# A streaming encoder layer on one core: the orders at both borders of its MLP are changed

## The chip, the cores and the metric

The kernel runs on one core of a Trainium2 chip. The metric is the device time of one execution in microseconds, the median of several runs. A core has five engines that work side by side and wait for each other through semaphores: TensorE (PE; its weight loads are PEld) multiplies matrices into PSUM, VectorE (DVE) and ScalarE (ACT) work element by element on SBUF and PSUM, GpSimd (POOL) does so on SBUF alone, and SyncE (SP) issues the transfers (DMA). Each engine takes its instructions in the order in which they stand for it.

## What is computed

One layer of an encoder on 1024 prompt rows and 64 sample rows of 1024 numbers: an input projection, three groups of heads, an output projection, a layer norm, and then the part that matters here, an MLP with a squared ReLU and the second norm:

```python
def sq_relu_mlp(x, w_up, w_down):
    h = jnp.square(jax.nn.relu(jnp.einsum('btd,df->btf', x, w_up)))
    return jnp.einsum('btf,fd->btd', h, w_down)
...
        xp = layer_norm(ALPHA * xp + mix, ln1_g[l], ln1_b[l])
        xp = layer_norm(ALPHA * xp + sq_relu_mlp(xp, w_up[l], w_down[l]), ln2_g[l], ln2_b[l])
```

w_up is 1024 x 4096, w_down 4096 x 1024; all numbers are float32.

## The kernel before

**Precision.** Each factor of a product is kept as two parts: a high half, which an activation on ScalarE rounds into the multiplier's format, and a low half, what is left, which `lo_sub` (L98) subtracts on VectorE or GpSimd. A product runs three passes of matmuls: high by high, high by low, low by high. Making both halves of an operand is called a split (`split`; its activation stands at L1232).

**Seven products for eight.** Both matrices of the MLP are cut in quarters and multiplied by a scheme with seven products, whose operands are sums and differences of quarters, of the data and of the weights, and whose results are added and subtracted to the four quarters of the result.

**Up.** The 4096 columns of w_up are taken in 16 pairs of blocks, p = 0 to 15, each with two chains: s = 0 (288 columns of x, the samples among them) and s = 1 (256). `prep(p)` (L1489) loads the weights (`up_load`, tile wr), splits three blocks as they are into tile wa (`wops` 0, 1 and 3, for the products 0, 1 and 5), makes four sums in place (`w_sums`, L1241 to L1245) and splits these into tile ws: `high` is the activation (L1514), `low` the subtraction. A `Chain` runs products 0 to 6 in PSUM banks A, B, C and D; after each, VectorE adds the result into the eight-part tile hh (L1308 to L1314). Product 6 goes into the bank D that product 3 had, so it waits until L1308, which follows product 4, has read it. `relu` (L1326) and `sums` (L1335 to L1338) make the operands of down, and SP stores them in DRAM (h4_dr, h3_dr, hs_dr; L1339 to L1343). At the end of up, c3 is the chain of p = 15 with s = 1, and c4 the one with s = 0, the last of all.

**Down.** 4096 rows of w_down are taken in 8 parts c, each with two groups g of rows of x: g = 2c and 2c + 1. For a part, `wd_load` loads two tiles of raw rows, `wd_split(c, q, n)` splits its seven operands n, and `wd_sum(c, q, k)` (L1426) makes the four differences k in place: difference 3 is what split 6 reads, and split 3 reads difference 2. For a group, `h_load` fetches operands of h (which = 0: four, which = 1: three) and `h_split(g, which, x)` splits them over a PSUM tile st (L1453, L1457, L1458). `Down` runs seven products for two blocks of rows x, in PSUM banks that VectorE adds into `acc` (L1721 for the first addition to a bank's result, L1723 for others). `acc_load` (L1469) fetches rows of x into acc first. `sample` does the 64 sample rows by way of the tile hs, loaded by `hs_load`; `b12_again` reloads one block of weights (rb) for it.

**Where tiles lie.** acc 2 and 6 (tile a26) take the place of c4's tile hh0, and acc 3 and 7 (a37) that of c3's hh1: they can be loaded when c4's or c3's stores are through. Raw rows of part 0, q = 1, lie in the tile awa, and so does half of group 1's operands (`hraw[0, 1]`, in the place of two of those raw blocks) and acc NB, the samples' rows. hx, the other half of group 1's operands, has held operands of group 0. acc 1, 4 and 5 lie where up's operand x lay, and can be loaded behind the last product of up.

**The order.** A scheduler with a model of times orders each engine's instructions, except inside `in_order`, where the order of the text is kept on every engine. The stretches that the change touches are inside: the chains of p = 1 with `prep(2)` (for p = 2 TensorE's order alone), the last three chains of up, and `first_group`, which is group 0 of down. What follows `first_group` is the scheduler's, so instructions of group 1 may stand among those of group 0, and a change in one place may move others behind it.

Of the kernel before, what the change touches and what calls it, by code (L numbers as in the profile page):

```python
# [12 lines left out]
F32 = mybir.dt.float32  # L13
# [7 lines left out]
P = 128  # L21
PASSES = ((0, 0), (0, 1), (1, 0))
D = 1024
# [33 lines left out]
def _build(nc, tc, a, es):  # L57
# [39 lines left out]
    def lo_sub(eng, out, src, hi):  # L97
        eng.tensor_tensor(out, src, hi.bitcast(F32), op=ALU.subtract)  # L98
# [1132 lines left out]
    def split(hi, lo, raw, eng):  # L1231
        nc.scalar.activation(hi, raw, AF.Copy)  # L1232
        lo_sub(eng, lo, raw, hi)
# [189 lines left out]
    def wd_sum(c, q, k, eng):  # L1423
        r = raws[c, q]
        o, x, y = ((0, 1, 0), (1, 3, 1), (3, 3, 0), (2, 2, 3))[k]
        eng.tensor_tensor(r[:, o], r[:, x], r[:, y], op=ALU.subtract)  # L1426
# [20 lines left out]
    def h_split(g, which, x, only=None, qs=(0, 1)):  # L1447

        for q in qs:
            t = h_tile(g, which, x)  # L1450
            o = 3 if which else 4
            raw = t[:, 1, q].bitcast(F32) if (g, which) == (0, 0) else hraw[which, q][:, :, x * P:(x + 1) * P]
            nc.scalar.activation(t[:, 0, q], raw, AF.Copy)  # L1453
            tag = (only or ("o", "tr"))[n_stage[0] % 2]
            n_stage[0] += 1
            st = ps.tile([P, 4, P], F32, name=f"st{n_stage[0]}", tag=tag, bufs=1 if tag in ("o", "tr") else 2)[:, 0:o]
            nc.scalar.activation(st, t[:, 0, q].bitcast(F32), AF.Copy)  # L1457
            nc.vector.tensor_tensor(t[:, 1, q], raw, st, op=ALU.subtract)  # L1458
# [17 lines left out]
    def two(t, tile_):  # L1476
        accf[t] = tile_
        acc[t, 0], acc[t, 1] = tile_[:, 0:512], tile_[:, 512:D]

    with p3:  # L1480
# [7 lines left out]
        def prep(p, rest=True, raw=None):  # L1488
            raw = raw or up_load(p)  # L1489
            pool = rp if p % 2 else lp  # L1490
            wa = pool.tile([P, 3, 2, 4, P], F32R, name=f"wa{p}", tag="wa")
            f0, f1 = raw[0:2]
            a, b = slice(0, 4), slice(4, 8)
            for o, src in ((0, f0[:, a]), (1, f0[:, b]), (2, f1[:, b])):
                split(wa[:, o, 0], wa[:, o, 1], src, nc.gpsimd)
            whole = len(raw) == 3
            parts = ((slice(0, 256), raw[2]),) if whole else ((slice(0, P), f0), (slice(P, 256), f1))

            wsp = []

            def summed(part=(0, 1)):
                w_sums(f0, f1, part)
                if 1 not in part:
                    return
                ws = pool.tile([P, 2, KT, 256], F32R, name=f"ws{p}", tag="ws")
                wsp.append(ws)
                wops[p].update({2: ws[:, :, b, 0:P], 4: ws[:, :, b, P:256],
                                5: ws[:, :, a, 0:P], 6: ws[:, :, a, P:256]})

            def high():  # L1510
                ws = wsp[0]
                for q in (a, b) if whole else (slice(0, 8),):
                    for c, src in parts:
                        nc.scalar.activation(ws[:, 0, q, c], src[:, q], AF.Copy)  # L1514

            def low():
                ws = wsp[0]
                for c, src in parts:
                    lo_sub(nc.vector, ws[:, 1, :, c], src, ws[:, 0, :, c])

            wops[p] = {0: wa[:, 0], 1: wa[:, 1], 3: wa[:, 2]}
            if rest:
                summed()
                high()
                low()
            return summed, high, low
# [98 lines left out]
        def products(c, some):  # L1625
            for i in some:
                c.product(i, False)

        with in_order(border):
            c1 = chain(NP - 2, 1)  # L1630
            products(c1, (0, 1))
            ch.relu()
            products(c1, (2,))
            ch.sums()
            products(c1, (3, 4))
            summed()
            high()
            products(c1, (5, 6))
            c2 = chain(NP - 2, 0)
            products(c2, (0, 1))  # L1640
            c1.relu()
            c1.sums()
            products(c2, (2,))
            low()
            wd_load(0, 0)
            products(c2, (3, 4, 5, 6))
            c3 = chain(NP - 1, 1)
            products(c3, (0,))

            h4 = lp.tile([P, 2, 2, 2, 4, P], F32R, name="h4a", tag="ws")  # L1650
            hbuf[0, 0], hbuf[0, 1] = h4[:, 0], h4[:, 1]
            for q in range(2):
                for x in range(2):
                    nc.sync.dma_start(h4[:, x, 1, q].bitcast(F32), h4_dr[q, 0][:, :, x * P:(x + 1) * P])
            awa = lp.tile([P, 3, D], F32, name="awa", tag="wa")
            hx = lp.tile([P, D], F32, name="hx", tag="hx")
            hraw[0, 0], hraw[0, 1] = (y.rearrange("p (o c) -> p o c", o=4) for y in (hx, awa[:, 1]))
            two(0, awa[:, 2])

            two(NB, awa[:, 0])  # L1660
            h_load(0, 1, 0)
            wd_load(0, 1, awa[:, 0:2].rearrange("p q (o c) -> p (q o) c", o=2))
            products(c3, (1,))
            c2.relu()
            products(c3, (2,))
            c2.sums()
            acc_load(0)
            products(c3, (3, 4))
            h_split(0, 0, 0, ("o", "s"))
            products(c3, (5, 6))  # L1670
            c4 = chain(NP - 1, 0)
            products(c4, (0,))
            slots = [big.tile([P, 8704], F32R, name=f"wd0_{q}", tag="xw") for q in range(2)]
            for q in range(2):
                wset[0][q] = slots[q][:, 0:7168].rearrange("p (h b c) -> p h b c", h=2, b=7)
                hbuf[1, q] = slots[q][:, 7168:8704].rearrange("p (h q o c) -> p h q o c", h=2, q=2, o=3)

            def both_pairs(n):
                for q in range(2):
                    wd_split(0, q, n, nc.gpsimd)  # L1680

            both_pairs(0)
            products(c4, (1,))
            h_split(0, 0, 1, ("o", "s"))
            both_pairs(2)
            for q in range(2):
                wd_sum(0, q, 0, nc.vector)
            products(c4, (2,))
            both_pairs(1)
            wd_sum(0, 0, 1, nc.vector)  # L1690
            products(c4, (3, 4))
            wd_sum(0, 1, 1, nc.vector)
            products(c4, (5,))
            h_load(0, 1, 1)
            for q in range(2):
                wd_sum(0, q, 2, nc.vector)
            h_split(0, 1, 0, ("tr", "s"))
            both_pairs(3)
            products(c4, (6,))
            both_pairs(4)  # L1700
# [3 lines left out]
    with ExitStack() as p3:  # L1704
# [173 lines left out]
        def first_group():  # L1878
            ch = [Down(0, x) for x in range(2)]

            def both(n):
                for d in ch:
                    d.product(n)
                for d in ch:
                    d.evac(n)

            for t in (1, 4, 5):
                acc_load(t)
            for q in range(2):
                wd_sum(0, q, 3, nc.vector)  # L1890
            both(0)
            for q in range(2):
                wd_split(0, q, 5, nc.gpsimd)
            h_split(0, 1, 1)
            h_load(1, 0, 0)
            both(1)
            for q in range(2):
                wd_split(0, q, 6, nc.gpsimd)
            for q in range(2):
                h_load(1, 1, q)  # L1900
            both(2)
            h_split(1, 0, 0, None, (0,))
            c4.relu()
            both(3)
            h_load(1, 0, 1)
            wd_load(1, 0)
            c3.relu()
            both(4)
            h_split(1, 0, 0, None, (1,))
            c3.sums(nc.gpsimd)  # L1910
            c4.sums()
            h_split(1, 0, 1)
            both(5)
            a37 = lp.tile([P, 2, D], F32, name="acc37", tag="hh1")
            two(3, a37[:, 0])
            two(7, a37[:, 1])
            for t in (2, 6, 3, 7, NB):
                acc_load(t)
            for k in range(3):
                wd_split(1, 0, k, nc.gpsimd)  # L1920
            both(6)
            wd_sums(1, 0, nc.gpsimd)
            wd_split(1, 0, 3, nc.vector)
            wd_split(1, 0, 4, nc.gpsimd)
            wd_split(1, 0, 5, nc.vector)
            wd_split(1, 0, 6, nc.gpsimd)
# [207 lines left out]
```

## Time and profile before

| | |
|---|---|
| three runs, us | 1390.9, 1392.92, 1397.63 |
| median, us | 1392.92 |
| profiled execution, us | 1389.83 |
| its span, first to last instruction, us | 1388.1 |
| granted TensorE clock, mean | 0.988 |
| up, us from the start of the span | about 672 to 1026 |
| down, us from the start of the span | about 1026 to 1388 |

The profile has a page for the whole execution and answers to questions: groups of instructions, waits, windows, a timeline and the chain of work that ended last. In a timeline row stand the start in us, the busy time, engine, line, operation, tiles written <- tiles read, shapes, the number of instructions merged and, in brackets, how long the engine was free before and what it waited for. In a row of waits stand the waiting engine, line and tile, what it waited for, the total in us, how often, and the longest. The lines that matter stand in the prediction.

### The profile page before, as it was taken

What the parts mean: (1) busy time and instruction counts of PE and PEld (TensorE: products, weight loads), DVE (VectorE), ACT (ScalarE), POOL (GpSimd) and SP (SyncE); (2) the same over time, 40 slices, a digit from 0 to 9 for tenths busy, and PEclk for the clock granted to TensorE, in tenths of its full rate; (3) what the DMA queues carried; (4) which work ended last, traced back from release to release, by engine and by line L of the source; (5) the groups of instructions that cost most, each with busy time, mean ns of one, the idle gap of its engine ahead of it and who ended that gap; (6) DMA issues with size and microseconds to landing.
All of it is one profiled execution on the core that took longest, in us unless ns stands there. A gap on an engine that the chain in (4) does not pass through costs nothing.

```text
span 1388.1 us, 24324 instructions
## 1 busy us (share of the span) xinstructions
PE 1322.0 (95%) x8827; PEld 1203.3 (87%) x8827; DVE 998.1 (72%) x1795; ACT 719.1 (52%) x1561; POOL 612.3 (44%) x667
## 2 busy tenths in 40 slices
PE   7999999999898998999999999999998999999996
PEld 7899989999888997877899999999986788887874
DVE  4577666576788379779866878767677677768677
ACT  4367566566556366334523222222266676767665
POOL 3231231256665446756412212212167675565547
PEclk9999999999999999999999999999999999999999
DMA  7445474231403247532234344344468334334333
GB/s 221 111 123 152 154 212 116 68 78 43 103 13 74 62 153 250 169 107 76 77 114 143 124 163 141 119 169 141 159 217 291 119 142 167 130 129 158 109 126 129
DMA packets 159088, 185.64 MB, mean 134 GB/s; under 512 B 27756, under 2 KB 117164, under 8 KB 158968
## 3 DMA queue, kind: packets, MB, share of 16 engines
q1 hardware_dynamic: 158968, 184.08, 41.7%
q8 instruction: 70, 1.15, 0.3%
q14 instruction: 50, 0.41, 0.1%
HBM read 117.65 MB, written 60.10 MB: 128 GB/s over the span
## 4 chain that ended last, share of the span: by engine, by line
PE 52%; DVE 15%; DMA 10%; ACT 9%; POOL 9%; issue 5%; SPq 0%; ACTq 0%; DVEq 0%; POOLq 0%
PE zA L1294 9%; PE zD L1294 6%; PE kvsb L362 5%; PE kvfox L362 4%; PE mx L251 4%; POOL wd L98 3%; PE zC L1294 3%; PE zB L1294 3%; PE A L1756 3%; DMA rd<-w_down 3%; POOL rd L1426 2%; DVE snsb L545 2%; DMA rwo<-w_out 2%; DMA awa<-h_dr 2%; DMA raw<-w_in 1%
## 5 line engine op out<-in xcount | busy, mean ns | idle before, releaser
L98 POOL TENSOR_TENSOR wa<-wr,wa 128x512 fp32r<-128x512 f32 x42 | 64.7, 1568 | 224.5 <-ACT wa L1232 224.5
L98 POOL TENSOR_TENSOR wd<-rd,wd 128x512 fp32r<-128x512 f32 x77 | 100.8, 1321 | 109.3 <-ACT wd L1232 109.1
L251 PE MATMUL mx<-xT,oTb 128*128 128x512 f32 (+1 forms) x416 | 104.4, 402 | 1.0 <-DVE oTb L98 1.0
L1294 PE MATMUL zA<-xo,ws 128*128 128x288 f32 (+1 forms) x720 | 98.6, 291 | 3.1 <-DVE ws L98 3.1
L1294 PE MATMUL zD<-xo,ws 128*128 128x288 f32 (+1 forms) x720 | 97.6, 289 | 2.6 <-DVE hh L1308 1.4
L1294 PEld LDWEIGHTS zA<-xo,ws 128*128 128x128 f32 x720 | 94.8, 191 | 3.3 <-DVE ws L98 3.3
L1294 PEld LDWEIGHTS zD<-xo,ws 128*128 128x128 f32 x720 | 93.5, 189 | 3.3 <-DVE hh L1308 1.9
L251 PEld LDWEIGHTS mx<-xT,oTb 128*128 128x128 f32 (+1 forms) x416 | 75.6, 187 | 19.5 <-DVE oTb L98 1.9
L1426 POOL TENSOR_TENSOR rd<-rd 128x512 f32<-128x512 f32 x56 | 79.5, 1419 | 29.4 <-DVE b L98 27.1
L547 POOL TENSOR_TENSOR sgsb<-sgsb,snsb 128x127 f32<-128x127 f32 (+7 forms) x48 | 58.5, 1219 | 75.7 <-DVE snsb L545 72.1
L362 PE MATMUL kvfox<-wkvfox,xT 128*128 128x256 f32 (+3 forms) x624 | 90.5, 293 | 1.1 <-ACT wkvfox L338 0.5
L362 PE MATMUL kvsb<-wkvsb,xT 128*128 128x256 f32 (+1 forms) x624 | 88.5, 287 | 0.0
L1232 ACT ACTIVATE wd<-rd 128x512 fp32r<-128x512 f32 x105 | 63.4, 623 | 47.3 <-POOL rd L1426 22.9
L1756 PE MATMUL A<-wd,wd 128*128 128x512 f32 x312 | 83.5, 396 | 3.2 <-DVE acc L1723 2.3
L362 PEld LDWEIGHTS kvfox<-wkvfox,xT 128*128 128x128 f32 (+1 forms) x624 | 81.6, 193 | 2.5 <-ACT wkvfox L338 0.9
L545 DVE TENSOR_TENSOR_SCAN snsb<-snsb,one 128x128 f32<-128x128 f32 (+7 forms) x48 | 72.5, 1514 | 15.3 <-ACT snsb L544 14.7
L362 PEld LDWEIGHTS kvsb<-wkvsb,xT 128*128 128x128 f32 (+1 forms) x624 | 79.5, 187 | 0.2
L1305 ACT ACTIVATE sn<-zA 128x256 f32<-128x256 f32 (+1 forms) x80 | 31.0, 390 | 93.2 <-PE zA L1294 82.2
L1756 PEld LDWEIGHTS A<-wd,wd 128*128 128x128 f32 x312 | 58.0, 188 | 19.6 <-DVE acc L1723 4.0
L1756 PE MATMUL A<-wd,h4a 128*128 128x512 f32 x240 | 64.7, 394 | 1.4 <-POOL wd L98 0.8
L1514 ACT ACTIVATE ws<-wr 128x1024 fp32r<-128x1024 f32 x28 | 29.2, 1056 | 58.4 <-DVE wr L1244 57.9
L1756 PEld LDWEIGHTS A<-wd,h4a 128*128 128x128 f32 x240 | 44.8, 188 | 13.0 <-POOL wd L98 1.2
(548 smaller groups left out, 3748.9 us busy)
## 6 DMA issues: line engine op xcount, KB each, us to landing
h_dr<-hh SPq DMA_DIRECT2D x30, 512.0 KB, 3.2
rd<-w_down SPq DMA_DIRECT2D x30, 512.0 KB, 4.4
wr<-w_up SPq DMA_DIRECT2D x13, 1024.0 KB, 5.5
hr<-h_dr SPq DMA_DIRECT2D x31, 384.0 KB, 4.5
h_dr<-hh SPq DMA_DIRECT2D x30, 384.0 KB, 3.8
raw<-w_in SPq DMA_DIRECT2D x44, 256.0 KB, 3.5
wo_dr<-swo SPq DMA_DIRECT2D x32, 256.0 KB, 2.5
xT<-wo_dr SPq DMA_DIRECT2D x8, 1024.0 KB, 8.0
```

Source lines behind the costliest of these rows:

```text
L98: eng.tensor_tensor(out, src, hi.bitcast(F32), op=ALU.subtract)
L251: nc.tensor.matmul(acc[0:m], oT[:, k, hx, 0:m], wo[k // 4][hw][:, k % 4, cs], start=(i == 0), stop=(i == len(seq) - 1))
L362: nc.tensor.matmul(acc[0:n, c0:c0 + n1 - n0], xT[k // 4][:, k % 4, c:c + n], wt[:, k, hw, n0:n1], start=(i == 0), stop=(i == len(seq) - 1))
L545: nc.vector.tensor_tensor_scan(g[:, 0:n][:, ::-1], g[:, 0:n][:, ::-1], one.broadcast_to([P, n]), 1.0, op0=ALU.mult, op1=ALU.bypass)
L547: nc.gpsimd.tensor_tensor(s[:, 0:n - 1], s[:, 0:n - 1], g[:, 1:n], op=ALU.mult)
L1232: nc.scalar.activation(hi, raw, AF.Copy)
L1294: nc.tensor.matmul(z, w[:, hw, k], xop(s, bo, hx)[:, k, :], start=(new and k == 0 and j == 0), stop=(k == 3 and j == 2), skip_group_check= ...
L1305: nc.scalar.activation(c, z, AF.Copy)
L1426: eng.tensor_tensor(r[:, o], r[:, x], r[:, y], op=ALU.subtract)
L1514: nc.scalar.activation(ws[:, 0, q, c], src[:, q], AF.Copy)
L1756: nc.tensor.matmul(z, h[:, hx, q, o], wset[self.c % 2][q][:, hw, wb], start=((n in (0, 3) or n == 1 and self.c == 0) and q == 0 and j == 0 ...
```

## The change

It has two places. In `prep`, for p = 2 alone, the three blocks of wa are split in the order 2, 1, 0, block 2's low half is made by VectorE instead of GpSimd, and the low half of the four sums is made in two pieces, the first half of the rows of all columns and then the second. At the border of up and down, h_split(0, 0, 1) moves from c4's first products to c3's product 5; c3's relu and sums move from group 0 of down to behind the first two weight splits in c4, and c4's to the head of the group, both on VectorE (c3's sums were on GpSimd); the rows of x for acc 3 and 7 are loaded first, those of 2 and 6 after product 1, the samples' after product 4, all of them formerly after product 5; and difference 3 with its split 6 moves behind product 2.

```diff
--- before.py
+++ after.py
@@ -1491,8 +1491,10 @@
             wa = pool.tile([P, 3, 2, 4, P], F32R, name=f"wa{p}", tag="wa")
             f0, f1 = raw[0:2]
             a, b = slice(0, 4), slice(4, 8)
-            for o, src in ((0, f0[:, a]), (1, f0[:, b]), (2, f1[:, b])):
-                split(wa[:, o, 0], wa[:, o, 1], src, nc.gpsimd)
+            blocks = ((0, f0[:, a]), (1, f0[:, b]), (2, f1[:, b]))
+
+            for o, src in blocks[::-1] if p == 2 else blocks:
+                split(wa[:, o, 0], wa[:, o, 1], src, nc.vector if p == 2 and o == 2 else nc.gpsimd)
             whole = len(raw) == 3
             parts = ((slice(0, 256), raw[2]),) if whole else ((slice(0, P), f0), (slice(P, 256), f1))
 
@@ -1515,8 +1517,9 @@
 
             def low():
                 ws = wsp[0]
-                for c, src in parts:
-                    lo_sub(nc.vector, ws[:, 1, :, c], src, ws[:, 0, :, c])
+                for q in (a, b) if p == 2 else (slice(0, 8),):
+                    for c, src in parts:
+                        lo_sub(nc.vector, ws[:, 1, q, c], src[:, q], ws[:, 0, q, c])
 
             wops[p] = {0: wa[:, 0], 1: wa[:, 1], 3: wa[:, 2]}
             if rest:
@@ -1667,7 +1670,9 @@
             acc_load(0)
             products(c3, (3, 4))
             h_split(0, 0, 0, ("o", "s"))
-            products(c3, (5, 6))
+            products(c3, (5,))
+            h_split(0, 0, 1, ("o", "s"))
+            products(c3, (6,))
             c4 = chain(NP - 1, 0)
             products(c4, (0,))
             slots = [big.tile([P, 8704], F32R, name=f"wd0_{q}", tag="xw") for q in range(2)]
@@ -1680,8 +1685,9 @@
                     wd_split(0, q, n, nc.gpsimd)
 
             both_pairs(0)
+            c3.relu()
+            c3.sums()
             products(c4, (1,))
-            h_split(0, 0, 1, ("o", "s"))
             both_pairs(2)
             for q in range(2):
                 wd_sum(0, q, 0, nc.vector)
@@ -1884,38 +1890,37 @@
                 for d in ch:
                     d.evac(n)
 
-            for t in (1, 4, 5):
+            a37 = lp.tile([P, 2, D], F32, name="acc37", tag="hh1")
+            two(3, a37[:, 0])
+            two(7, a37[:, 1])
+            for t in (3, 7, 1, 4, 5):
                 acc_load(t)
-            for q in range(2):
-                wd_sum(0, q, 3, nc.vector)
+            c4.relu()
+            c4.sums()
             both(0)
             for q in range(2):
                 wd_split(0, q, 5, nc.gpsimd)
             h_split(0, 1, 1)
             h_load(1, 0, 0)
             both(1)
-            for q in range(2):
-                wd_split(0, q, 6, nc.gpsimd)
+            for t in (2, 6):
+                acc_load(t)
             for q in range(2):
                 h_load(1, 1, q)
             both(2)
+            for q in range(2):
+                wd_sum(0, q, 3, nc.vector)
+            for q in range(2):
+                wd_split(0, q, 6, nc.gpsimd)
             h_split(1, 0, 0, None, (0,))
-            c4.relu()
             both(3)
             h_load(1, 0, 1)
             wd_load(1, 0)
-            c3.relu()
             both(4)
             h_split(1, 0, 0, None, (1,))
-            c3.sums(nc.gpsimd)
-            c4.sums()
             h_split(1, 0, 1)
+            acc_load(NB)
             both(5)
-            a37 = lp.tile([P, 2, D], F32, name="acc37", tag="hh1")
-            two(3, a37[:, 0])
-            two(7, a37[:, 1])
-            for t in (2, 6, 3, 7, NB):
-                acc_load(t)
             for k in range(3):
                 wd_split(1, 0, k, nc.gpsimd)
             both(6)
```

On each engine this gives the following order. TensorE has the same 8829 instructions; at the second border their order is the same up to product 3 of group 0, and then two matmuls of group 1 that stood ahead of product 4 stand behind it, together with a third. On VectorE, L1308 of c4 stands behind c3's L1326 and L1335 to L1338 and three differences (L1426); c4's five follow its L1314, ahead of the second half of h_split(0, 1, 1) and of the first L1721. On ScalarE the activations of split 6 stand behind those of h_split(0, 1, 1), and between the two of them stands that of rb; the activation of hx for group 1 follows, then the second rb, then hs, and then the half of group 1's operands in awa. GpSimd has 667 instructions for 672. On SP c3's two stores stand ahead of hr, and acc 3, 7, 1, 4, 5, c4's three stores, hx, rb twice, acc 2 and 6, hr twice, hs twice and awa follow in this order.

## The prediction

> **What bounds the kernel now.** I read the page's busy times first, then the windows, then TensorE's own waits.
>
> ```profile
> span 1388.1 us, 24324 instructions
> PE 1322.0 (95%) x8827; PEld 1203.3 (87%) x8827; DVE 998.1 (72%) x1795; ACT 719.1 (52%) x1561; POOL 612.3 (44%) x667
> ```
>
> TensorE is the bound: 1322.0 of 1388.1 us. The number of matmuls is the same after the change, so only TensorE's gaps can be won, and only a new gap can cost. The windows show where gaps are in the MLP.
>
> ```profile
> 727.00:731.00 4.00, 1.03 (x9) 0.80 (x7) 3.21 (x5) 1.15 (x2) 0.00 (x0) 0.96 0.00 0
> 731.00:734.40 3.40, 3.31 (x15) 3.31 (x16) 3.21 (x7) 0.65 (x2) 0.00 (x0) 0.54 0.60 182
> 1057.00:1067.00 10.00, 6.76 (x26) 4.36 (x25) 8.84 (x14) 4.61 (x10) 4.10 (x5) 1.00 1.05 368
> 1100.00:1150.00 50.00, 50.00 (x219) 40.23 (x218) 39.38 (x61) 38.56 (x78) 31.41 (x25) 1.00 0.41 147
> ```
>
> The columns are the stretch, its length, busy time of PE, PEld, DVE, ACT and POOL, the granted clock and DMA. Behind the borders (1100 to 1150) TensorE is never free: a delay at a border is a delay at the end, us for us. The second row matters as well: just after the gap at 727 to 731 the clock is 0.54, so this gap is paid for twice. The gaps by releaser, at the first border and from 1010 to 1070 us:
>
> ```profile
> PE zA L1294 <- DVE ws L98: 3.1, 1, 3.1
> PE A L1756 <- DVE acc L1721: 2.3, 2, 1.6
> PE zD L1294 <- DVE h4a L1458: 1.2, 1, 1.2
> PE D L1756 <- DVE acc L1721: 0.8, 1, 0.8
> PE zD L1294 <- DVE hh L1308: 0.7, 1, 0.7
> PE A L1756 <- DVE awa L1721: 0.6, 1, 0.6
> PE A L1756 <- ACT h4a L1453: 0.5, 1, 0.5
> ```
>
> That is 3.1 us at the first border and 6.1 us at the second: the change cannot win more than these 9.2 us and the clock behind the first.
>
> **First border (weights of chain 2, p == 2).**
>
> ```profile
> 719.32 1.66 ACT L1232 ACTIVATE wa<-wr 128x512 fp32r<-128x512 f32 x3
> 720.02 3.80 POOL L98 TENSOR_TENSOR wa<-wr,wa 128x512 fp32r<-128x512 f32 x3 [25.17 <-ACT wa L1232]
> 723.85 0.69 DVE L1241 TENSOR_TENSOR wr<-wr 128x512 f32<-128x512 f32 x1 [3.97 <-POOL wa L98]
> 728.74 2.29 DVE L98 TENSOR_TENSOR ws<-wr,ws 128x2048 fp32r<-128x2048 f32 x1 [0.79 <-ACT ws L1514]
> 721.68 3.19 PE L1294 MATMUL zA<-xo,wa 128*128 128x288 f32 x24
> 731.09 4.51 PE L1294 MATMUL zA<-xo,ws 128*128 128x288 f32 x23 [3.06 <-DVE ws L98]
> ```
>
> Before, the sums start at 723.85, when POOL has read all three blocks, and the third product waits 3.06 us for one low half of 2.29 us. Its 23 matmuls take 4.51 us where 24 in the first product take 3.19: 23/24 of that is 3.06, so 1.45 us went to the clock. Border one costs 4.5 us.
>
> After: VectorE takes block 2 itself (one operation of 0.69, as L1241), so the first sum need not wait for POOL, and the low half comes in two pieces of about 1.15. But the blocks run backwards, 2, 1, 0, and the first product, at 721.68, reads block 0 from its second matmul. POOL's two operations (3.80 / 3 = 1.27 each) begin after two of ScalarE's three activations, 719.32 + 1.1 = about 720.5, so block 0's low half comes at 723.1; with one VectorE sum let in between, which reads two SBUF operands as POOL does (priced below), at 723.6. TensorE stands there from 721.8: a new wait of 1.3 to 1.9, taken 1.8. Then L1244 (0.7), an activation of half the columns (1.1), L1312 and the first low piece (1.15) end near 727.2; the third product, moved to 729.5, finds it ready. The 3.06 us are gone, 1.8 stand two products earlier. The clock did not drop at the 1.6 us wait (1.00 from 1057 to 1067) and did at 3.06: I charge a third of 1.45. Term: -4.5 + 1.8 + 0.5 = **-2.2**, bounds -3.2 and -1.2.
>
> [...]
>
> **Second border, end of up.**
>
> ```profile
> 1018.20 1.90 PE L1294 MATMUL zD<-xo,ws 128*128 128x288 f32 x12 [1.16 <-DVE h4a L1458]
> 1021.51 1.74 PE L1294 MATMUL zC<-xo,wa 128*128 128x288 f32 x12
> 1023.98 1.86 PE L1294 MATMUL zD<-xo,ws 128*128 128x288 f32 x12 [0.72 <-DVE hh L1308]
> 1011.59 0.60 ACT L1457 ACTIVATE st<-h4a 128x512 f32<-128x512 f32 x1
> 1018.66 1.50 DVE L1426 TENSOR_TENSOR rd<-rd 128x512 f32<-128x512 f32 x1
> 1020.09 1.77 DVE L1426 TENSOR_TENSOR awa<-awa 128x512 f32<-128x512 f32 x1
> 1021.77 1.78 DVE L1426 TENSOR_TENSOR rd<-rd 128x512 f32<-128x512 f32 x1
> 1023.48 0.45 DVE L1308 TENSOR_TENSOR hh<-zD,hh 128x288 f32<-128x288 f32 x1
> 1014.91 1.29 POOL L98 TENSOR_TENSOR wd<-rd,wd 128x512 fp32r<-128x512 f32 x1 [30.86 <-ACT wd L1232]
> ```
>
> The split h_split(0,0,1) now stands in c3, so c4's fourth product no longer waits for its bank: 1.16 us, with the refill 1.3, leave the first row, and TensorE comes to up's last product (1021.51 + 1.59 - 1.3) at 1021.8. That product waits for L1308, which stands in VectorE's order behind three weight differences, and c3's relu and four sums are now put ahead of those. What these cost beside POOL's splits is shown at 771 to 776:
>
> ```profile
> 771.57 0.42 DVE L1338 TENSOR_TENSOR hh<-hh 128x256 f32<-128x256 f32 x1
> 771.90 1.22 DVE L1326 SCALAR_TENSOR_TENSOR hh<-hh 128x1024 f32<-128x1024 f32 x1
> 773.04 1.51 DVE L1336 TENSOR_TENSOR hh<-hh 128x256 f32<-128x256 f32 x1
> 774.47 1.50 DVE L1335 TENSOR_TENSOR hh<-hh 128x256 f32<-128x256 f32 x1
> 772.11 5.00 POOL L98 TENSOR_TENSOR wa<-wr,wa 128x512 fp32r<-128x512 f32 x3 [14.01 <-ACT wa L1232]
> ```
>
> A sum of 0.42 alone takes 1.5 while POOL works, and POOL's three take 5.00 instead of 3.80: they take turns. ScalarE's four activations for the moved split follow 1011.59 + 0.60 and end about 1014.6; with its subtraction and L1314 VectorE reaches the relu at 1015.5, just when POOL's six splits begin (their activations 0.6 later than in the POOL row). From there: relu 1.2, four sums at 1.43 (774.47 - 773.04) 5.7, L1310 0.4; five of POOL's six are then through, so the differences take 1.4 + 0.6 + 0.6. Sum 9.9: L1308 at 1025.4, the last product at 1025.9 against 1023.98. With sums of 0.42 and differences as before (4.8) it is 1024.1; with a turn lost by the relu too, 1027.2. Taken 1026.2: **+2.2**, bounds +0.1 and +3.2. The wait is then 4.4 us, longer than the 3.06 that dropped the clock: **+1.45**, bounds 0 and 2.9 (two such windows).
>
> [...]
>
> **Second border, down's first groups.**
>
> ```profile
> 1026.95 11.88 POOL wd L98 x8
> 1038.85 4.35 DMA awa<-h_dr
> 1048.75 4.21 DMA hs_dr<-hh
> 1053.10 5.04 DMA acc<-x_dr
> ```
>
> The chain of waits shows what the change goes for: c4's stores leave late (1048.75), acc 2 and 6 may only be loaded into that tile behind them (1053.10), and the 2.3 and 0.8 us waits for L1721 follow. With relu and sums ahead of the group the loads leave before 1045: these 3.1 us go, and the 0.6 and 0.5 with them: -4.2.
>
> ```profile
> 1032.94 1.77 DVE L1721 SCALAR_TENSOR_TENSOR awa<-awa,p 128x512 f32<-128x512 f32 x1
> 1037.72 0.68 DVE L1721 SCALAR_TENSOR_TENSOR acc<-acc,A 128x512 f32<-128x512 f32 x1
> acc<-hs_dr SPq DMA_DIRECT2D x2, 64.0 KB, 8.1
> ```
>
> What comes for it. (a) c4's relu and sums (1.35 + 1.7 to 5.7) now stand before the additions, beside POOL's next six splits; the differences k=3 (2 x 0.6 to 1.8) leave. The additions need 4.8 us (1032.94 to 1037.72): with the shift from above they end 1037 to 1042.2, TensorE wants the fifth product at 1040: wait 0 to 2.2, taken 1.5. (b) k=3 now runs behind these additions, near 1042, so both splits n=6 end near 1047 instead of 1038.83. The load of awa waits for the second on SP (it writes that half), then 4.35 us. ScalarE has the split of hx for group 1 behind the n=6 activations, too: TensorE, which has three matmuls of group 1 between products five and six, waits about 2 us there (0 to 3). (c) awa's half lands near 1052; ScalarE's order puts the samples' split (hs) ahead of it, whose loads stand on SP behind acc 2, acc 6 and two hr, and land 8.1 after issue. TensorE comes to these matmuls at about 1051 and waits 1 to 5 us; taken 3.5. Against that -4.2: **+2.8**, bounds -2.2 and +6.
>
> Loads of acc 3 and 7 come before 1, 4 and 5 on SP, two of 512 KB more; needed from 1036, the first leave at 1024 behind c3's stores: hidden. The order in other groups changes under the scheduler; at 50.00 of 50.00 I give it nothing, bounds -1 and +2.
>
> **Sum:** -2.2 + 2.2 + 1.45 + 2.8 = +4.3 against the profiled execution, 1389.83 us (span 1388.1 and 1.7 around it): 1394.1. That execution lies 3.1 below the median shown, 1392.92, so on the median's footing 1397.2.
>
> **The rivals.** *The gaps simply close.* If VectorE gets its turns first, or POOL is later than I think, L1308 is done before 1021.8 (alone: 1.2 + 1.7 + 0.4 + 2.0 from 1015.5 is 1020.8), and awa and hs land in time: -3.2 - 2.2 - 4.2 and 0.6 left over, -9.0: 1383.9. For it: the cause of each wait is really taken away. Against: the rows at 773. *A pile-up on ScalarE.* hs's loads hold the in-order ScalarE, with them every split of group 1. It decides once hs lands after 1053: 4 us more than in (c), the clock drops there and at the first border (2 x 1.45), the relu loses its turn (1.2): +12.4, 1405. For it: 8.1 us to land, and stores that must land before acc 2 may be issued. Against: loads issue earlier, with the queue less full. *The first border's wait only moves*, since block 0 comes last: 1.9 and a clock drop leave -1.2 there, and the second border breaks even: 1391.7.
>
> **How the numbers follow.** Forecast 0.45, pile-up 0.24, gaps close 0.23, moved and even 0.08. 0.5% of 1392.92 is 7.0 us, about what a measurement of this kernel can tell from no change. Of the forecast (its own range 1391 to 1404) 0.18 lies above 1399.9; with the pile-up slower is 0.42. Of "gaps close" 0.20 is below 1386: faster 0.20. Same: the rest, 0.38. The range, 1386 to 1406, holds all but half of the fast case.
>
> **What would show it.** Right: zA of chain 2 waits 1.3 to 1.9 us for POOL wa in its first product, no wait for ws; up's last zD waits over 3 us for L1308, L1335 to L1338 beside it at about 1.5, a clock near 0.5 behind; PE waits for h4b or ACT between 1041 and 1055; no wait for acc 2. Wrong: sums at 0.42 there, the last zD without a wait, or PE free of gaps by 1050.

## The result, and the profile after

The changed kernel takes 1397.62 us (median of 17 runs, 1395.62 to 1403.24), the one before 1392.48 (17 runs, 1387.56 to 1397.63). The ratio is 1.0047, interval 1.0036 to 1.0059: 0.36% to 0.59% slower, or 5.0 to 8.2 us of 1392.48. The forecast was 1397.2.

The page of after, the span and the busy times:

```profile
span 1397.1 us, 24306 instructions
PE 1327.8 (95%) x8827; PEld 1206.7 (86%) x8827; DVE 1004.9 (72%) x1801; ACT 718.4 (51%) x1561; POOL 605.9 (43%) x662
```

The profiled execution of after took 1398.85 us. TensorE's busy time rose by 5.8 us with the same number of matmuls, so part of the difference is clock. Some of that lies ahead of the change: from 55 to 63 us and from 303 to 309 us the granted clock is 0.79 and 0.72 in after and 1.00 in before. TensorE's waits of after, first from 720 to 740 us, then from 1000 to 1110:

```profile
PE zA L1294 <- POOL wa L98: 1.6, 1, 1.6
PE zD L1294 <- DVE hh L1308: 5.1, 1, 5.1
PE A L1762 <- DVE awa L1727: 2.0, 1, 2.0
PE A L1762 <- DVE h4b L1458: 1.0, 1, 1.0
PE A L1762 <- DVE h4a L1458: 0.8, 1, 0.8
```

Every wait of before that the change went for is gone: the 3.1 us for ws, 1.2 for h4a ahead of zD, and those for acc 2 and 6. Others stand in their place. (The lines of after are numbered 6 higher in down.)

**First border.** Timeline of after:

```profile
724.62 0.69 DVE L98 TENSOR_TENSOR wa<-wr,wa 128x512 fp32r<-128x512 f32 x1
725.35 1.67 DVE L1241 TENSOR_TENSOR wr<-wr 128x512 f32<-128x512 f32 x1
725.18 2.96 POOL L98 TENSOR_TENSOR wa<-wr,wa 128x512 fp32r<-128x512 f32 x2 [25.66 <-DMA h_dr<-hh]
726.32 0.29 PE L1294 MATMUL zA<-xo,wa 128*128 128x288 f32 x1
728.19 3.15 PE L1294 MATMUL zA<-xo,wa 128*128 128x288 f32 x23 [1.58 <-POOL wa L98]
```

TensorE stops after one matmul, because block 0's low half is the second of POOL's two operations, and goes on when POOL ends at 728.14. VectorE's first sum took 1.67 instead of 0.69 beside POOL, and POOL 2.96 instead of 2.53 (two thirds of 3.80). What the clock did is shown below.

**End of up.** Timeline of after, VectorE, POOL and TensorE:

```profile
1017.48 2.22 DVE L1326 SCALAR_TENSOR_TENSOR hh<-hh 128x1024 f32<-128x1024 f32 x1
1019.73 1.40 DVE L1335 TENSOR_TENSOR hh<-hh 128x256 f32<-128x256 f32 x1
...
1023.92 1.48 DVE L1338 TENSOR_TENSOR hh<-hh 128x256 f32<-128x256 f32 x1
1025.32 0.45 DVE L1310 TENSOR_TENSOR hh<-zB,sn 128x288 f32<-128x288 f32 x1
1025.69 1.38 DVE L1426 TENSOR_TENSOR rd<-rd 128x512 f32<-128x512 f32 x1
1028.19 0.45 DVE L1308 TENSOR_TENSOR hh<-zD,hh 128x288 f32<-128x288 f32 x1
1018.57 2.27 POOL L98 TENSOR_TENSOR wd<-awa,wd 128x512 fp32r<-128x512 f32 x1
1028.69 3.14 PE L1294 MATMUL zD<-xo,ws 128*128 128x288 f32 x12 [5.07 <-DVE hh L1308]
```

From the relu's start to L1308's is 10.7 us (1017.48 to 1028.19). Each sum costs a POOL operation's length, 1.4 where 0.42 is its own time, and the relu loses about 1.0. POOL pays too: the operation beside the relu takes 2.27. The last product waits 5.07 us, and its 12 matmuls then take 3.14 where before took 1.86.

**Down's first groups.** Timeline of after:

```profile
1039.11 1.51 DVE L1338 TENSOR_TENSOR hh<-hh 128x256 f32<-128x256 f32 x1
1044.25 0.68 DVE L1727 SCALAR_TENSOR_TENSOR awa<-awa,A 128x512 f32<-128x512 f32 x1
1045.08 0.94 PE L1762 MATMUL A<-wd 128*128 128x512 f32 x3 [2.05 <-DVE awa L1727]
1045.85 2.70 PE L1762 MATMUL A<-wd,wd 128*128 128x512 f32 x6
1053.73 0.53 ACT L1232 ACTIVATE hs<-acc 128x128 fp32r<-128x128 f32 x2 [3.41 <-DMA acc<-hs_dr]
1055.20 0.63 ACT L1453 ACTIVATE h4b<-awa 128x512 fp32r<-128x512 f32 x1 [0.95 <-DMA awa<-h_dr]
1056.77 0.69 DVE L1458 TENSOR_TENSOR h4b<-awa,st 128x512 fp32r<-128x512 f32 x1 [3.34 <-ACT st L1457]
1057.28 0.63 PE L1762 MATMUL A<-wd,h4b 128*128 128x512 f32 x2
1059.38 0.97 PE L1762 MATMUL A<-wd,h4a 128*128 128x512 f32 x3 [0.78 <-DVE h4a L1458]
```

c4's sums hold back the additions, and the bank A comes free 2.05 us late. ScalarE does wait 3.41 us for hs and then for awa; but TensorE comes to that half's matmuls only at 1057.28 and finds it ready. It loses 0.78 at the split that stands behind it in ScalarE's queue.

The windows behind the three longest waits of after (1.58 us at the first border, 5.07 and 2.05 at the second), with the granted clock in the third column from the right:

```profile
728.00:731.00 3.00, 2.81 (x22) 2.81 (x23) 2.79 (x5) 1.48 (x2) 0.14 (x1) 1.00 0.00 0
1028.60:1032.00 3.40, 3.31 (x13) 3.27 (x14) 3.27 (x8) 2.53 (x6) 0.89 (x1) 0.54 0.90 278
1046.00:1049.50 3.50, 3.50 (x11) 2.58 (x10) 0.73 (x2) 2.49 (x5) 2.43 (x2) 0.53 1.02 356
```

1.00 behind the 1.58 us of the first border, 0.54 behind the 5.07 and 0.53 behind the 2.05: the second border pays the clock twice.

**Where the time went.** Every profile here records 8827 matmuls. The lag in the table is the start of a kernel's matmul number k, counted from its first instruction, less the start of number k, likewise, in the shown profile of before. A part's change is the difference of two lags: first border between k = 4800 and 5200 (695 and 751 us in before), second between 7300 and 7900 (1016 and 1158), later groups from 7900 to 8820 (to 1376).

```
kernel                  lag at 4800  first border  second border  later groups   sum
after                        +4.66        -2.86         +5.09         +2.04     +4.3
after, again (e10)           +1.69        -2.80         +5.92         +3.28     +6.4
before, again (e12)          +0.72        +0.15         -1.79         -0.32     -2.0
e1  first border alone       +2.12        -2.84         +0.40         -0.63     -3.1
e2  second border alone      +1.96        +0.16         +5.30         +1.72     +7.2
e3  POOL without reads       +2.35        -2.87         -1.14         +3.20     -0.8
e4  block 0 second           +0.66        -4.47         +4.84         +2.87     +3.2
e5  c3's sums sooner         +1.72        -2.81         +2.74         +2.94     +2.9
e6  c4's sums later          -0.67        -2.84         +6.63         -0.73     +3.1
e7  all three                +0.06        -4.49         +5.41         +0.28     +1.2
e8  first border, 2 0 1      -2.27        -4.45         +0.58         +2.21     -1.7
e11 the same, again          +0.42        -4.52         -1.19         +0.12     -5.6
e9  sums apart               +4.77        -4.50         +3.20         +2.03     +0.7
```

The first column is work that the change doesn't touch, and varies from -2.3 to +4.8. Of the 9.0 us between the two shown executions (1398.85 and 1389.83) 4.66 are of this kind. The two profiles of after less the two of before give (4.27 + 6.40)/2 - (0 - 1.96)/2 = +6.3, within the measured 5.0 to 8.2.

### The profile page after: what moved, and what is told of

It is laid out like the page before. It is cut to its first block, busy times and chain, and to the rows that moved or that the text cites. A ratio compares the mean times of both kernels' runs of the same rounds, so it can differ in the third digit from the quotient of the medians.

```text
span 1397.1 us, 24306 instructions
## 1 busy us (share of the span) xinstructions
PE 1327.8 (95%) x8827; PEld 1206.7 (86%) x8827; DVE 1004.9 (72%) x1801; ACT 718.4 (51%) x1561; POOL 605.9 (43%) x662
## 4 chain that ended last, share of the span: by engine, by line
PE 55%; DVE 13%; DMA 10%; ACT 8%; POOL 7%; issue 6%; SPq 1%; ACTq 0%; DVEq 0%; POOLq 0%
PE zA L1294 9%; PE zD L1294 6%; PE kvsb L362 5%; PE A L1762 5%; PE mx L251 4%; PE zB L1294 3%; PE zC L1294 3%; PE kvfox L362 3%; PE D L1762 2%; DMA rwo<-w_out 2%; DMA rd<-w_down 2%; POOL wd L98 2%; POOL rd L1426 1%; PE qsb L503 1%; DVE snsb L545 1%
## 5 line engine op out<-in xcount | busy, mean ns | idle before, releaser
L1426 POOL TENSOR_TENSOR rd<-rd 128x512 f32<-128x512 f32 x56 | 79.8, 1426 | 30.7 <-DVE b L98 28.4
L547 POOL TENSOR_TENSOR sgsb<-sgsb,snsb 128x127 f32<-128x127 f32 (+7 forms) x48 | 58.4, 1218 | 76.1 <-DVE snsb L545 68.9
```

Of the source, the lines that this page charges most:

```text
L547: nc.gpsimd.tensor_tensor(s[:, 0:n - 1], s[:, 0:n - 1], g[:, 1:n], op=ALU.mult)
```

## The experiments

**e1 and e2: each border alone.** e1 is before with the two edits in `prep`; e2 is after without them.

```diff
-            for o, src in ((0, f0[:, a]), (1, f0[:, b]), (2, f1[:, b])):
-                split(wa[:, o, 0], wa[:, o, 1], src, nc.gpsimd)
+            for o, src in blocks[::-1] if p == 2 else blocks:
+                split(wa[:, o, 0], wa[:, o, 1], src, nc.vector if p == 2 and o == 2 else nc.gpsimd)
...
+                for q in (a, b) if p == 2 else (slice(0, 8),):
```

> The kernel before with the change of prep alone (block order 2, 1, 0, block 2's low half on VectorE, low in two pieces). Theory (the two borders add up; block 0's low half comes last and is waited for): chain 2's first product waits 1.3 to 1.9 us for POOL wa, no product waits for ws, the clock stays at 1.0, and from there on everything is 2.8 us earlier than before: about 1389.7, ratio 0.998. Rival (the first border's wait only moves on, to a later chain or to the end of up): the lead of 2.8 us is lost again before the last chain, ratio 1.000.

> The changed kernel with prep as before. Theory: the 3.06 us wait for ws and the slow clock behind it are back at the first border, and the second border costs what it does in the changed kernel: a wait of 4 to 5.5 us for L1308 before up's last product and about 2 us for awa before product 4, in all 7 to 8 us more than before: about 1400, ratio 1.0055. Rival (the loss comes from later groups that the scheduler orders anew, not from the border): the start of the first matmul behind 1100 us is less than 2 us later than before.

A ratio is to the runs of before that were made beside the experiment; their medians are 1391.26 us for e1 to e4, 1390.12 for e5 to e8 and 1391.09 for e9 to e12.

e1: 1387.23 us (9 runs), ratio 0.9971, 0.9960 to 0.9981. e2: 1398.97 (5 runs), ratio 1.0051, 1.0033 to 1.0070. In e2 the wait of 3.1 us for ws is back, and the wait of 5.1 for L1308 stays; the waits behind it are spread otherwise than in after (1.1 for awa, 1.6 and 1.0 for h4b). In e1 the first border's wait is 1.6 for POOL, and the lag doesn't move at the second border by more than before's own does. The first border gains, the second loses more, and neither needs the other. The predicted direction of each part is shown.

**e3: POOL without reads.** What if POOL's first six splits of down read nothing? The low halves of operands 0, 1 and 2 of part 0 are left out: set to zero.

```diff
+        if c == 0 and n < 3:
+            nc.scalar.activation(w[:, 0, b], raws[c, q][:, src], AF.Copy)
+            nc.gpsimd.memset(w[:, 1, b].bitcast(F32), 0.0)
+            return
```

> The changed kernel, but GpSimd fills the low halves of the splits n = 0, 1, 2 of part 0 with zeros instead of subtracting (the low parts of these three weight blocks are left out, so its output lacks them); VectorE's instructions are the same. Theory (VectorE and GpSimd take turns where both read from SBUF with two operands): with no reads by GpSimd c3's relu takes 1.2 to 1.3 and its sums 0.42 each, L1308 of c4 comes 5 us earlier, and the wait before up's last product falls from 5.1 to below 1 us. Rival (there is simply too much VectorE work ahead of L1308, or its operands are late): the sums stay at 1.4 and the wait at 4 to 5 us.

1391.47 us in one run. Timeline of e3:

```profile
1015.16 1.23 DVE L1326 SCALAR_TENSOR_TENSOR hh<-hh 128x1024 f32<-128x1024 f32 x1
1016.42 0.42 DVE L1335 TENSOR_TENSOR hh<-hh 128x256 f32<-128x256 f32 x1
1020.20 0.46 DVE L1308 TENSOR_TENSOR hh<-zD,hh 128x288 f32<-128x288 f32 x1
1011.84 2.40 POOL L1415 MEMSET wd<- 128x512 f32 x5 [0.89 <-PE zD L1294]
1024.50 2.15 DVE L1326 SCALAR_TENSOR_TENSOR hh<-hh 128x1152 f32<-128x1152 f32 x1
1026.69 1.40 DVE L1335 TENSOR_TENSOR hh<-hh 128x256 f32<-128x256 f32 x1
1037.38 1.15 PE L1766 MATMUL A<-wd 128*128 128x512 f32 x3 [3.60 <-DVE awa L1731]
```

With POOL through at 1014.2, relu and sums have their own times, 1.23 and 0.42, L1308 starts 5.0 us behind the relu instead of 10.7, and the last product doesn't wait. c4's sums, where POOL's next splits still read, cost 1.40 each as in after, and TensorE now stands for the additions behind them, 3.60 us, as it comes to them sooner. The wait at the end of up is contention with POOL, shown; and taking it away uncovers the next one. The edit also shortens POOL's own work, but that is not what VectorE gained by: in after it runs from the relu to L1308 without a pause, and of the 5.7 us that e3 saves there the sums are 4.0, the relu 1.0 and the first difference 0.7. In this one kernel the same instruction takes 0.42 with POOL through and 1.40 beside its reads.

**e4: block 0 second.** Order 2, 0, 1 instead of 2, 1, 0.

```diff
-            for o, src in blocks[::-1] if p == 2 else blocks:
+            for o, src in (blocks[2], blocks[0], blocks[1]) if p == 2 else blocks:
```

> The changed kernel with the blocks of chain 2 split in the order 2, 0, 1. Theory (the 1.58 us wait at chain 2's first product is block 0's place in GpSimd's order): the wait for POOL wa falls to 0 to 0.4 us in the first product, the second may wait up to 0.3 for block 1, and all behind it is 1.2 to 1.6 us earlier. [...]

1393.76 us in one run; TensorE has no wait from 715 to 740 us. Timeline of e4:

```profile
721.23 2.99 POOL L98 TENSOR_TENSOR wa<-wr,wa 128x512 fp32r<-128x512 f32 x2 [25.69 <-DMA h_dr<-hh]
722.37 3.37 PE L1294 MATMUL zA<-xo,wa 128*128 128x288 f32 x24
```

TensorE's 24 matmuls run through (3.37 us, 3.19 in before), with POOL's first operation ready in time. The first border gains 4.47 instead of 2.86: the 1.6 us that the new wait cost, seen four times more, in e7, e8, e9 and e11 (4.45 to 4.52).

**e5, e6: the sums at other places.** In e5 c3's relu and sums come right behind c3's last product, ahead of h_split(0, 0, 1) and POOL's splits; in e6 c4's come behind product 2 and difference 3 of group 0, and the loads of acc 2 and 6 behind awa's.

```diff
# e5
-            products(c3, (5,))
+            products(c3, (5, 6))
+            c3.relu()
+            c3.sums()
             h_split(0, 0, 1, ("o", "s"))
-            products(c3, (6,))
...
-            c3.relu()
-            c3.sums()
# e6
-            c4.relu()
-            c4.sums()
             both(0)
...
                 wd_sum(0, q, 3, nc.vector)
+            c4.relu()
+            c4.sums()
```

> The changed kernel, with c3's relu and sums right behind c3's last product and ahead of h_split(0, 0, 1) on VectorE. Theory (the wait before up's last product is the turns that relu and sums take with GpSimd's splits): they run at 1015.4 to 1018.5 by the changed kernel's clock, before GpSimd's splits have got far; at most two sums take over 1 us, L1308 comes at about 1024 instead of 1028.2, the wait falls from 5.1 to 0.5 to 1.5, with no clock drop behind it. The wait before product 4 stays near 2. Rival (L1308 is late because of the three weight differences, which GpSimd's splits release): the wait stays above 3 us.

> The changed kernel, with c4's relu and sums behind product 2 and difference 3, and the loads of acc 2 and 6 behind that of awa. Theory (product 4 waits because c4's relu and sums stand ahead of the first additions): the wait for awa before product 4 falls from 2.0 to 0 to 0.5, without the second clock drop; difference 3 comes 2 us sooner; acc 2 and 6 are still in time, so no wait of over 0.5 us for them behind; 2.5 to 4 us less at the end of the border. Up's last product waits its 5.1 us as before. Rival (the additions wait for ScalarE's late half of h_split(0, 1, 1), or the later loads bring the old 3.1 us back): the wait for awa stays above 1.5, or waits for acc of over 1 us come between 1060 and 1080.

e5: 1394.45 us in one run. The wait for L1308 is gone, but h_split(0, 0, 1), now behind the sums, keeps TensorE 2.2 us (1.2 in before), and the granted clock is 0.62 from 1018.19 to 1022.50 us, where no drop was expected. Two of the four sums still fall beside POOL's splits. The additions to awa come 2.3 us late as in after; the second border costs 2.74 instead of 5.1 to 5.9. e6: 1392.56 in one run, but its second border is the worst of all, +6.63, where 2.5 to 4 us less than after's were expected. The wait for awa is gone, two for h4b stand there: 3.0 for the low half, which now queues behind the sums on VectorE, and 1.3 for its activation, which stands on ScalarE behind three others, the first of them held by the load of rb. The granted clock is 0.51 from 1021.2 to 1028.1 us, at the same wait of 5.07 for L1308 as in after, and 0.51 again from 1045.1 to 1052.0: twice as long as in after each time (3.4 us at 0.54, 3.5 at 0.53), with TensorE still waiting in the first 2.1 and 0.9 us of it; the time of the run is low for its later groups (-0.73) and its start (-0.67).

**e7 and e9: put together.** e7 is after with the edits of e4, e5 and e6. e9 is before with the first border of e4, c3's sums as in e5, and c4's relu and sums together behind product 2, with the loads of acc 2 and 6 ahead of the next weights and those of acc 3 and 7 behind 1, 4 and 5; difference 3 and its splits stay as before.

```diff
# e9, against before with the first border in order 2, 0, 1
             products(c3, (5, 6))
+            c3.relu()
+            c3.sums()
...
             c4.relu()
+            c4.sums()
             both(3)
             h_load(1, 0, 1)
+            for t in (2, 6):
+                acc_load(t)
             wd_load(1, 0)
-            c3.relu()
...
-            c3.sums(nc.gpsimd)
-            c4.sums()
```

> The changed kernel with block order 2, 0, 1 and both of the moves of c3's and c4's sums. Theory: the first border gives 4.4 us against the kernel before; at the second the waits before the last product (under 1.5) and before product 4 (under 0.5) are small and the old waits for acc stay away: 1 to 4 us less than before there; the groups behind 1200 us lose up to 2 as in the changed kernel. In all 4 to 7 us less than before: 1384 to 1388, ratio 0.995 to 0.997. Rival (waits at this border only change places): no less than before at the second border, ratio 0.997 or above, and not better than the first border's change alone.

> Before with the first border in order 2, 0, 1, and of the second border this much: c3's relu and sums stand behind c3's product 6 on VectorE, c4's relu and sums together behind product 2 of down's group 0, ahead of product 3, acc 3 and 7 are loaded behind 1, 4 and 5, acc 2 and 6 ahead of the next weights. Difference 3, its splits, group 1's operands and the order of h_split(0,0,1) stay as before. Theory (what costs is c4's block of sums ahead of group 1's splits, and the late difference 3): the waits for acc 2 and 6 shrink from 3.4 us to under 1, a wait for awa, h4a or h4b of 1 to 3 us comes where the sums stand ahead of additions, up's last product waits 1 us or less; second border between -2 and +1 us against the kernel before, total with the first border's -4.5: 1384 to 1387 on the footing of 1390.1. Rival (any block of c4's sums inside group 0 costs a wait and a dropped clock): a wait of 3 us or more between 1030 and 1050 us with the clock half, second border +3 or worse, 1388 or more.

e7: 1390.49 us (12 runs), ratio 0.9999, 0.9986 to 1.0011: level with before. e9: 1391.32 (12 runs), ratio 1.0005, 0.9989 to 1.0020. For both the rival holds: at the second border e7 loses more (+5.41), and e9 most (+3.20), of the 4.5 us that the first one gains. Timelines of e7 and then of e9:

```profile
1035.83 1.35 DVE L1326 SCALAR_TENSOR_TENSOR hh<-hh 128x1152 f32<-128x1152 f32 x1
1041.66 0.67 DVE L1458 TENSOR_TENSOR h4b<-hx,st 128x512 fp32r<-128x512 f32 x1
1042.39 0.80 PE L1761 MATMUL A<-wd,h4b 128*128 128x512 f32 x1 [4.07 <-DVE h4b L1458]
```

```profile
1019.81 3.25 PE L1294 MATMUL zD<-xo,ws 128*128 128x288 f32 x12 [2.47 <-DVE h4a L1458]
1040.74 1.35 DVE L1326 SCALAR_TENSOR_TENSOR hh<-hh 128x1152 f32<-128x1152 f32 x1
1045.69 1.27 DVE L1726 SCALAR_TENSOR_TENSOR acc<-acc,D 128x512 f32<-128x512 f32 x2
1046.41 1.26 PE L1761 MATMUL D<-wd 128*128 128x512 f32 x3 [3.62 <-DVE acc L1726]
```

c4's relu and sums hold VectorE for 5 us (e9) to 8.3 (after) wherever they stand as one block in group 0, and what TensorE wants next stands behind them: the additions to awa in after (2.05), the split of h4b in e7 (4.07), the additions to D in e9 (3.62). Before had split them up, with TensorE's work in between; VectorE in the timeline of before:

```profile
1038.92 1.35 DVE L1326 SCALAR_TENSOR_TENSOR hh<-hh 128x1152 f32<-128x1152 f32 x1
1040.19 1.28 DVE L1721 SCALAR_TENSOR_TENSOR acc<-acc,D 128x512 f32<-128x512 f32 x2
1044.52 0.69 DVE L1458 TENSOR_TENSOR h4b<-awa,st 128x512 fp32r<-128x512 f32 x1 [0.72 <-ACT st L1457]
1045.13 0.42 DVE L1335 TENSOR_TENSOR hh<-hh 128x256 f32<-128x256 f32 x1
```

**e8: the first border alone in order 2, 0, 1.** Before with e4's `prep`.

> The kernel before with prep's change and block order 2, 0, 1, its second border left alone. Theory: no wait over 0.3 us at the first border, 4.4 to 4.6 us less than before from there to the end, ratio 0.9965 to 0.997. Rival (part of the gain is lost where the scheduler orders later groups): under 3.5 us in the profile's matmul starts at the end.

1386.86 us (12 runs), ratio 0.9975, 0.9963 to 0.9986: faster than both kernels. By times it can't be told from e1 (0.9971); by the lags its first border gains 1.6 us more.

**e10, e11, e12: after, e8's kernel and before once more.** No edit.

> The changed kernel once more, to see how far a single profile's lag in down's later groups can be trusted. Theory (the scheduler's other order there costs 2.0 us, by ScalarE's late preloads of bank B): the lag grows by 1.5 to 2.5 us again between matmuls 7900 and 8820, with the waits for ACT B at the same places; first border -2.8 and second +5.1 again, each within 0.4. Rival (it varies from one execution to the next): the lag there grows by less than 1 or by more than 3.

> The first border alone in order 2, 0, 1, once more; behind the first border its instructions are those of before, yet its profile lost 2.2 us between matmuls 7900 and 8820. Theory (the kernel's order sets that loss): 2.2 again within 0.5. Rival (variation of the execution): anything between -0.5 and +2.5, other than the first.

> The kernel before once more, the footing of all lags. Theory: its lag against its own first profile changes by under 0.5 us at either border, and by under 0.5 in down's later groups. Rival: down's later groups vary by 1 us or more in the same kernel, so that a part of that size cannot be told from one profile.

One run each: 1397.97, 1384.83 and 1388.59 us. The first border repeats within 0.16. The second does not for the same kernel: before differs by 1.79 between its two profiles, in the waits for acc 2 and 6 (2.3 and 0.8 in the first, 1.4 and 0.5 in the second). E8's differs by 1.77, of which 1.5 come at the end of up: in the first profile TensorE waits 2.17 us for h4a, in the second 0.97, and 0.91 for L1308. That is 0.29 less; the other 1.2 would be a clock drop behind the longer wait, the author's estimate. After's differs by 0.83. Behind 7900 the rivals of e10 and e11 hold: after's kernel lost 3.28 where 1.5 to 2.5 were expected, and e8's lost 2.21 once and 0.12 once with before's instructions, so about 2 us there can't be laid to an order by one profile. Kernels with after's order of group 0 and its head lost 2.04, 3.28, 1.72 and 2.87 (after twice, e2, e4); those with before's order 0, -0.32, -0.63, 2.21 and 0.12. That is 2.5 against 0.3 on the mean: an order effect is likely, not settled. What it looks like in after, near 1218 us, timeline of after and then of before:

```profile
1218.02 0.58 ACT L1750 ACTIVATE B<-awa 128x512 f32<-128x512 f32 x1
1218.65 1.66 PE L1762 MATMUL B<-wd,h4a 128*128 128x512 f32 x6 [0.83 <-ACT B L1750]
```

```profile
1207.59 0.58 ACT L1744 ACTIVATE B<-awa 128x512 f32<-128x512 f32 x1
1210.50 1.55 PE L1756 MATMUL B<-wd,h4a 128*128 128x512 f32 x6
```

The copy into bank B ends 2.3 us ahead of its matmul in before, and just behind TensorE's arrival in after. Undoing that one step alone was not tried.

## Why the prediction was right

**First border, -2.2, measured -2.8 to -2.9.** The new wait was foreseen at its place, with 1.8 us, and took 1.58. The third of a clock drop (0.5) was not needed. With both right the term is -4.5 + 1.6 = -2.9.

**End of up, +2.2, measured +2.9.** TensorE came to the last product at 1023.62, which is 1021.8 less after's lag of 1.82 there, as foreseen. The product starts at 1028.69, or 1026.9 less that lag, against 1023.98. The place, the turns and the size of the sums (1.43 foreseen, 1.40 to 1.48 measured) were right. The relu's lost turn, which the prediction left to its upper bound, came: 2.22 instead of 1.2. So the start lies between the 1026.2 taken and the bound of 1027.2, which holds that turn.

**The clock behind it, +1.45, measured about +1.6:** 3.14 - 1.86 for the last product and 3.24 - 2.91 for the next.

**Down's first groups, +2.8, measured +0.6 and +1.5:** the rest of the second border, 5.09 - 2.9 - 1.6 in the first profile and 5.92 less lags up to k = 7400 of 4.43 in the second. All three places were right, the sizes not. (a) took 2.05 for 1.5, and a clock drop that the prediction didn't charge (6 matmuls in 2.70 instead of 1.53). (b) took 0.97 for 2, and (c), with the split behind it, 0.78 for 3.5. The step that failed in (c) is "TensorE comes to these matmuls at about 1051". The matmul at this place in the order, number 7442, starts at 1047.49 in before, and with the 3.65 of the end of up added that is 1051.1; the waits (a) and (b), which come ahead of it and which the sum itself counts with 3.5, are not in it. Awa's half was there at 1055.2, or 1053.4 less the lag of 1.82, somewhat behind the 1052 foreseen; but TensorE came at 1057.28, or 1055.5, and didn't wait for it. A wait behind other waits was counted as if they were not there. ScalarE was held by hs as said, 3.41 us, without a pile-up.

**Later groups, 0, measured +2.0 and +3.3,** at and over the bound of +2. "At 50.00 of 50.00 I give it nothing" took busy windows for a proof that no wait can come: from 1200 to 1250 us TensorE of after is busy for 49.17, with the wait for bank B in that stretch. Terms too small and too large cancelled in the sum of +4.3; the profiles say +4.3 and +6.4 and the runs 5.0 to 8.2. The places of the waits were foreseen; that the time came out at 1397.6 for a forecast of 1397.2 is luck, since down's first groups, which cost 1.3 to 2.2 less than their term, met later groups that cost 2.0 to 3.3 more. One sentence on the chances doesn't fit them: a range from 1386 leaves out the whole fast case of 0.20, not half of it.

**The rivals.** *The gaps simply close* needed sums that run free of POOL; e3 makes that for c3's sums, and its second border costs nothing (-1.14, less than what before differs by), yet gains nothing sure either, as c4's sums keep the gap open. *A pile-up on ScalarE* didn't come: hs landed at 1053.7, which less the lag of 1.82 is 1051.9, ahead of its point of 1053, and TensorE wasn't there yet. *The first border's wait only moves* is wrong by its gain in e1.

## What to carry to other kernels

When VectorE work is moved earlier to release a transfer, ask first whose reads it will run beside and what TensorE wants next from the same queue: the sums took their own 0.42 us beside nothing and 1.4 beside POOL, and as one block they kept TensorE waiting at each of the three places tried. In a chain of waits, carry the lateness of each into the arrival at the next, since a later arrival hides the next wait. Where one edit holds two independent parts, measure them apart: the first border alone is 0.25% to 0.29% faster than before, and the whole is 0.47% slower.

## What was not expected of the hardware

Behind a wait of 2.05 us (after) the granted clock was 0.53, behind waits of 1.57 (before) and 1.58 (after) it was 1.00. In e10, behind a wait of 1.95 and three matmuls, six matmuls took 2.53 us; the same six took 1.53 in before. Yet two waits of 2.22 us, both for h4a at the end of up, differ. The windows of e7 (its wait and what follows) and then of e5 (what follows its wait):

```profile
1012.60:1014.90 2.30, 0.08 (x2) 0.04 (x1) 2.30 (x4) 1.45 (x3) 2.30 (x2) 1.00 0.44 173
1014.90:1018.30 3.40, 3.40 (x25) 3.40 (x26) 3.40 (x4) 0.00 (x0) 3.40 (x4) 1.00 0.73 242
```

```profile
1018.19:1022.50 4.31, 4.31 (x21) 4.31 (x22) 4.31 (x5) 0.00 (x0) 4.31 (x4) 0.62 0.85 266
```

From the first start to the last end the 24 matmuls behind the wait take 3.48 us in e7 and 5.01 in e5, 1.53 more behind a wait of the same length. So here the length of the wait alone doesn't tell whether it is paid twice; what else decides was not shown, and no run was made to test it.

In after, where the sums ran beside POOL's splits, both took longer, and the shorter instruction by the larger share: a sum's 0.42 became 1.40 to 1.51, more than tripled, and POOL's splits of 1.27 rose to 1.44 to 1.49. The relu, about as long as a split (1.22), took 2.22 beside POOL and 1.23 without it (e3), and POOL's split beside it 2.27. At 771.90 in before the relu had kept its 1.22. There it began ahead of POOL's operation (772.11), in after behind it (1017.48 against 1017.31).
